# Low halves of sixteen weight blocks made early, stored, and loaded by casting transfers

## The chip, the core and the metric

The kernel runs on one NeuronCore of a Trainium2 chip. Five engines with queues of their own work side by side: TensorE (PE, with its weight loads shown as PEld) multiplies, VectorE (DVE) and ScalarE (ACT) do elementwise work, GpSimd (POOL) issues the indirect and the casting transfers, and SyncE (SP) issues the plain ones. The metric is device time in microseconds (us) of one execution.

## The reference

One decoder layer for 512 prompt rows and 64 sample rows (576 in all) of width 1024:

```
z  = rmsnorm(x) @ w_in                      # q, k, v, su, sv, gate_a, gate_b
A  = windowed attention(q, k, v);  B = gelu(su) * spatial_gate(layernorm(gelu(sv)))
h  = sigmoid(gate_a) * (A @ w_branch_a) + sigmoid(gate_b) * (B @ w_branch_b)
x1 = x + h @ w_out
x2 = x1 + peer(rmsnorm(x1))                 # 128*128 experts, 8 heads, top 16 each
x3 = x2 + sigmoid(rmsnorm(x2) @ w_ple_gate) * (p @ w_ple)

peer: q = xb @ w_q; scores against two sets of 128 keys; top 16 of each, top 16 of their sums
      out = sum over the 16 experts of a head: softmax gate * gelu(u[idx] . xb) * v[idx]
```

## The kernel before

**Split products.** Products run in fp32r. Each 128x1024 weight block is loaded in fp32 (`w_raw`), ACT rounds it into a high half (`w_hi`, line 66), DVE subtracts to get the low half (`w_lo`, line 67), and PE sums three products for each 128 rows of depth (`tform`, line 82): high by high, high by low of the activations, low by high. So a block is 24 matmuls. `load_block` (line 69) does this for every block, with four raw buffers and three of each half.

**Stages.** 30 blocks of `w_in` with attention and the gating unit beside them; the branch products (8 blocks `w_br`) and the output product (8 blocks `w_out`); 16 blocks of the retrieval queries (`peer_wq`) with the key scores; then the experts. The 16384 experts are handled in two ways. For 384 of the 576 rows the kernel multiplies by all experts in 128 first-stage blocks (`stage1`: `peer_uT[j]`, 24 matmuls of 384 columns, then gelu) and 128 second-stage blocks (`stage2`: `peer_v`, 18 matmuls of 512 columns), with a dense matrix of gates that `build_g` makes from one-hot products. For the other 192 rows (64 sample rows and 128 prompt rows) it gathers each chosen expert's row of u and v by an indirect transfer on POOL's queue (`gather_row`, line 721) and lets DVE multiply (lines 733 and 740): 384 rows in all, into five buffers (`row`).

**Retrieval.** `retrieve` is a generator of DVE steps (top 16, decoding of positions), run for five groups of rows. Groups 0 and 1 give the indices of the gathers; group 2 is the first that `build_g` needs, by way of `make_ew` (line 797), which transposes its results on PE (line 799). While groups 0 to 2 are retrieved, first-stage blocks are put between the steps, up to `S1_TOPK` = 4, 9 and 13 blocks in all. Then the loop over `tb` (24 times 16 tokens) brings the blocks up to a goal, calls `make_ew` for group 2 at `tb` 0, and runs `build_g`. In the loop over j the remaining first-stage blocks run between second-stage blocks; `SPILL`, the even blocks 2 to 38, have their results parked in DRAM and read back.

**Pace of the gathers.** `pay` adds a credit per step and gathers a row for each whole credit: 0.5 for a first-stage block during retrieval, 2.0 or 3.5 for a `tb`, 1.65 for a first-stage block in the loop over j, and `G2` (1.6 while first-stage blocks are left, then 2.0) for each j. At j = 112 the first 128 must be done, and at j = 122 (`TAIL1`) all that are left are issued.

**What sets the order.** The program text gives priorities. A planner of the framework walks the program with estimated durations, lets every engine take the ready instruction of highest priority, and so fixes each engine's order before the run; on the chip each engine keeps that order and waits by semaphores. `high_priority` lifts the splits of weights ahead of other work. An instruction that waits for a buffer or a result holds everything behind it on its engine or its queue.

```python
    for ti in range(3):
        for _ in retrieve(ti, ti < 2):
            if len(acts) < S1_TOPK[ti]:
                stage1()
        ...
        while len(acts) < goal:
            stage1()
        if tb == 0:
            make_ew(*found[2])
        build_g(tb)
```

Of the kernel before, what the change touches and what calls it, by code (L numbers as in the profile page):

```python
# [7 lines left out]
F32 = mybir.dt.float32  # L8
# [9 lines left out]
P = 128  # L18
# [3 lines left out]
KC = 8  # L22
# [9 lines left out]
ONE = (1, 2)  # L32
TAIL0 = 112
TAIL1 = 122
S1_TOPK = (4, 9, 13)
TBK = 7
S1_END = 6
RING = 44
# [2 lines left out]
TILES = [(512, 64), (0, 128), (128, 128), (256, 128), (384, 128)]  # L41
HALVES = (slice(0, 256), slice(256, 576))
EPS = 1e-6
STARTS = [0, 16, 24, 29, 33, 36, 38, 40, 42, 43, 44, 45, 46, 47, 48, 49]


@with_exitstack
def tile_decoder_step(ctx: ExitStack, tc: tile.TileContext, a, o):
# [20 lines left out]
    def load_block(src, shape=(P, KC, P), urgent=True):  # L69
# [5 lines left out]
            split(raw, hi, lo)  # L75
        return hi, lo

    def tform(ps, w, x, wk=0, nk=KC):
        n, i = 3 * nk, 0
        for k in range(nk):  # L80
            for wi, xi in ((0, 0), (0, 1), (1, 0)):
                mark_pe[0] = T.matmul(ps, lhsT=w[wi][:, wk + k, :], rhs=x[xi][k], start=i == 0,  # L82
                                   stop=i == n - 1)
                i += 1
# [15 lines left out]
    x1d = dr.tile([KC, P, NB], F32, name="x1d")  # L100
    pld = dr.tile([NT, D], F32, name="pld")
    ad = dr.tile([NSP, P, NB], F32, name="ad")
    gd = dr.tile([NJ // JB, P, NB // TB, JB, TB], F32, name="gd")

    psBs = ExitStack()
# [385 lines left out]
    for g in range(4):  # L491
        split(suT[:, g, :], mh[:, g, :], ml[:, g, :])
    e2s.close()
    ple(TILES[:3])
    ahl = [[t[:, g, :] for g in range(4)] for t in (ah, al)]
    mhl = [[t[:, g, :] for g in range(4)] for t in (mh, ml)]
    hs = ([], [])
    for c in range(KC):
        w = load_block(a["w_br"][c])
        for i, (x, k0_) in enumerate(((ahl, 0), (mhl, 4))):  # L500
            sg = sgs[2 * c + i]
            joint(w, x, lambda ps, cols: V.tensor_tensor(sg[:, cols], sg[:, cols], ps, op=ALU.mult), k0_, 4,
                  (mm, lambda: bank("sc"))[i])
        ga = tt()
        V.tensor_tensor(ga, sgs[2 * c], sgs[2 * c + 1], op=ALU.add)
        if c % 4 == 0:
            h4 = [f4(F32R), f4(F32R)]
        for h, t in zip(hs, h4):
            h.append(t[:, c % 4, :])
        split(ga, hs[0][c], hs[1][c])  # L510

    gp = pool(ctx, "gp", 2)
    rows = ExitStack()
    rowp = pool(rows, "rowp", 5)

    def row(shape=(P, D), dt=F32):
        return rowp.tile(list(shape), dt, name="row")

    x1 = f8(f4)
    xg = (f8(x4), f8(x4))  # L520
# [1 line left out]
    for c in range(KC):  # L522
        w = load_block(a["w_out"][c])
        xc = tt()
        S.dma_start(xc, a["xT"][c])
        joint(w, hs, lambda ps, cols: V.tensor_tensor(x1[c][:, cols], ps, xc[:, cols], op=ALU.add))
        S.dma_start(x1d[c], x1[c][:, P:512])
        gcol = vecs[:, 8 + c:9 + c]
        A.activation(xg[0][c], x1[c], AF.Copy, scale=gcol)
        V.scalar_tensor_tensor(xg[1][c], x1[c], gcol, xg[0][c].bitcast(F32), op0=ALU.mult, op1=ALU.subtract)  # L530
        if c:
            add(c - 1, x1[c - 1])
# [243 lines left out]
    def stage1():  # L776
        nonlocal j1, nlive
        j = j1
        j1 += 1
        w = load_block(a["peer_uT"][j])  # L780
        ps = (mm() if j % 2 or phase[0] > 1 else bank("pv"))[:, :NB]
        tform(ps, w, xb)
        if j in SPILL:
            act = held_x[-1][:, sorted(SPILL).index(j) % 6, :]
        else:
            n = nlive % RING
            nlive += 1
            act = held_x[n // 6][:, n % 6, :] if n < NXP - 6 else (
                acp[0][:, n - NXP + 6, :] if n < RING - 6 else held_x[-1][:, n - RING + 6, :])
        A.activation(act, ps, AF.Gelu_apprx_tanh)  # L790
        acts[j] = act
        if j in SPILL:
            S.dma_start(ad[sorted(SPILL).index(j)], act)
        pay(GP[phase[0]])
# [57 lines left out]
    for tb in range(NB // TB):  # L852
        if tb == TBK:
            for i, r_ in enumerate(rest_t):
                for _ in r_:
                    pass
                make_ew(*found[5 - len(rest_t) + i])
            tks.close()
            late = pool(aLs, "aL", 1, "right")
            acp.append(late.tile([P, RING - NXP, NB], F32, name="aL"))  # L860
            g0 = late.tile([P, JB, TB], F32, name="g0")
        if tb < TBK:
            goal = S1_TOPK[2] + (tb + 1) * (S1_PRE - S1_TOPK[2]) // TBK
        else:
            goal = S1_PRE + (tb - TBK + 1) * (NSP + RING - 1 - S1_END - S1_PRE) // (NB // TB - TBK)
        while len(acts) < goal:
            stage1()
        if tb == 0:
            make_ew(*found[2])
        build_g(tb)  # L870
        for _ in range(2):
            if rest_t and next(rest_t[0], 1) == 1:
                rest_t.pop(0)
                make_ew(*found[4 - len(rest_t)])
        pay(GT[tb >= TBK] if tb < 22 else 0)
# [79 lines left out]
    for j in range(NJ):  # L955
        for jb in (2, 4) if j == 0 else (j + 4,):
            if jb in SPILL:
                back[jb] = d3.tile([P, NB], F32, name="x1c")
                S.dma_start(back[jb], ad[sorted(SPILL).index(jb)])
        if j and j - 1 not in SPILL and j1 < NJ:  # L960
            stage1()
        pay(G2[0] if j1 < NJ else G2[1])
        if j == TAIL0:
            aLs.close()
            xds.close()
            spp.append(pool(sps, "spare", 2, "right"))
            gather(max(0, P - done[0]), mark_pe[0])
            pg = gp.tile([P, D], F32, name="xr")
            S.dma_start(pg, a["ple_g"])
            tails.append(gathered(0))  # L970
        if j == TAIL1:
            gather(1000, mark_pe[0])
        if j == NJ - 2:
            tails.append(gathered(1))
        if j % JB == 0:
            gsl = gsp[(j // JB + 1) % 2].tile([P, NB // TB, JB, TB], F32, name="gs")
            nb = NB // TB if j else NB // TB - 1
            with tc.high_priority(offset=0 if j else 300):
                S.dma_start(gsl[:, :nb], gd[j // JB][:, :nb])
            if j == 0:  # L980
                A.activation(gsl[:, nb], g0, AF.Copy)
        vw = load_block(pv_view[j], (P, D))
        wf = acts.pop(j)
        if j in SPILL:
            wf = back.pop(j)
        wfv = wf.rearrange("p (b t) -> p b t", t=TB)
        V.tensor_tensor(wfv, wfv, gsl[:, :, j % JB, :], op=ALU.mult)
        wh = d2.tile([P, NB], F32R, name="wh")
        wl = d2.tile([P, NB], F32R, name="wl")
        split(wf, wh, wl)  # L990
        held.append((j, wh, wl, *vw))
        if j != NJ - 2:
            for t in range(3):
                for hj in held:
                    stage2(t, *hj)
            held.clear()
        if max(SPILL) < j <= max(SPILL) + KC:
            add_x1(j - max(SPILL) - 1)
# [150 lines left out]
```

## Time and profile before

| what | us |
|---|---|
| median of three runs | 1764.56 |
| these runs | 1764.26 to 1765.45 |
| the profiled execution | 1767.91 |
| its span, first to last instruction | 1766.1 |
| PE busy in the span | 1741.2 |
| DVE busy | 1436.6 |
| ACT busy | 868.3 |
| POOL busy | 518.3 |

In the profile, busy times are counted in one execution. A PE that is busy all the time tells that its queue never ran dry, so what can be gained is in the gaps and in stretches of lower clock. An idle time carries the name of what ended it. The granted clock is given as a share of full speed; the two levels are 2.4 GHz and 1.2 GHz, so a mean of 0.83 over a stretch says that a third of it ran at the lower one.

### The profile page before, as it was taken

How to read it: one execution, taken by the hardware profiler on the slowest of the kernel's cores; microseconds unless marked ns; L12 is line 12 of the kernel's file. 1: busy time of each engine (PE TensorE's matmuls, PEld its weight loads, DVE VectorE, ACT ScalarE, POOL GpSimd, SP SyncE). 2: the span in 40 equal slices, each digit the busy share in tenths (PEclk: the TensorE clock that was granted, in tenths of full speed). 3: DMA queues.
4: the chain of work that ended last, by engine and by line, in shares of the span. 5: the costliest groups of instructions: out<-in, count | busy, mean ns of one | idle time of the engine just before them, and what ended most of it. 6: DMA issues, size and time to landing. Idle time of an engine off the chain costs nothing.

```text
span 1766.1 us, 27818 instructions
## 1 busy us (share of the span) xinstructions
PE 1741.2 (99%) x10118; PEld 1574.5 (89%) x10118; DVE 1436.6 (81%) x2878; ACT 868.3 (49%) x1526; POOL 518.3 (29%) x390
## 2 busy tenths in 40 slices
PE   8999999999999899999999999999999999999999
PEld 8987999999999899999988888899999899887777
DVE  6355556549899999999898899998888888999963
ACT  6567443344335698998833333333333333333441
POOL 0000000000002112455245454454544544566300
PEclk9999999999999999999999999999999999999999
DMA  7211224443227577999999999999999999999832
GB/s 238 93 49 48 72 93 135 142 151 97 81 92 235 170 245 238 361 350 349 345 397 359 374 393 405 395 410 361 364 333 365 361 340 325 340 375 375 289 127 78
DMA packets 176601, 457.07 MB, mean 259 GB/s; under 512 B 15568, under 2 KB 77008, under 8 KB 174416
## 3 DMA queue, kind: packets, MB, share of 16 engines
q1 hardware_dynamic: 120880, 253.22, 40.9%
q0 software_dynamic: 55584, 202.07, 30.8%
q8 instruction: 79, 1.29, 0.3%
q14 instruction: 58, 0.48, 0.1%
HBM read 420.18 MB, written 35.78 MB: 258 GB/s over the span
## 4 chain that ended last, share of the span: by engine, by line
PE 81%; issue 6%; DVE 5%; DMA 4%; POOL 3%; ACT 1%; SPq 0%; POOLq 0%; DVEq 0%; ACTq 0%
PE mm L82 36%; PE oacc L951 24%; PE pv L82 5%; POOL row L721 3%; PE oacc L916 2%; PE sc L836 2%; PE pt L836 2%; DMA row<-peer_u,idx 2%; DMA row<-peer_v,idx 2%; PE sc L82 1%; DVE w_lo L67 1%; PE sc L594 1%; PE pv L461 1%; PE mm L916 1%; PE pv L329 1%
## 5 line engine op out<-in xcount | busy, mean ns | idle before, releaser
L66 ACT ACTIVATE w_hi<-w_raw 128x1024 fp32r<-128x1024 f32 x325 | 344.0, 1059 | 367.9 <-PE mm L82 265.5
L721 POOL DMA_INDIRECT row<-peer_u,idx x192 | 260.2, 1355 | 861.6 <-issue 515.2
L67 DVE TENSOR_TENSOR w_lo<-w_raw,w_hi 128x1024 fp32r<-128x1024 f32 x325 | 396.6, 1221 | 80.1 <-ACT w_hi L66 77.2
L82 PE MATMUL mm<-xd,w_hi 128*128 128x384 f32 x1552 | 405.7, 340 | 0.5 <-ACT w_hi L66 0.5
L721 POOL DMA_INDIRECT row<-peer_v,idx x192 | 256.6, 1337 | 240.5 <-DVE acc L740 215.2
L82 PE MATMUL mm<-x,w_hi 128*128 128x320 f32 (+1 forms) x1504 | 305.4, 297 | 0.0
L82 PEld LDWEIGHTS mm<-xd,w_hi 128*128 128x128 f32 x1552 | 281.3, 189 | 6.0 <-ACT w_hi L66 0.8
L82 PE MATMUL mm<-xd,w_lo 128*128 128x384 f32 x776 | 263.8, 340 | 1.6 <-DVE w_lo L67 1.6
L82 PEld LDWEIGHTS mm<-x,w_hi 128*128 128x128 f32 x1504 | 239.3, 188 | 12.5 <-issue 9.0
L740 DVE SCALAR_TENSOR_TENSOR acc<-row,wts,acc 128x1024 f32<-128x1024 f32 x192 | 245.7, 1279 | 2.1 <-DMA row<-peer_v,idx 1.6
L951 PE MATMUL oacc<-w_hi,wl 128*128 128x512 f32 x768 | 241.5, 396 | 2.3 <-DVE wl L67 2.3
L951 PE MATMUL oacc<-w_hi,wh 128*128 128x512 f32 x768 | 242.0, 395 | 1.3 <-ACT wh L66 1.3
L733 DVE SCALAR_TENSOR_TENSOR row<-row,xr 128x1024 f32<-128x1024 f32 x192 | 231.5, 1219 | 12.5 <-DMA row<-peer_u,idx 12.4
L951 PE MATMUL oacc<-w_lo,wh 128*128 128x512 f32 x768 | 241.5, 395 | 0.0
L82 PE MATMUL mm<-x,w_lo 128*128 128x320 f32 (+1 forms) x752 | 220.6, 294 | 0.0
L951 PEld LDWEIGHTS oacc<-w_hi,wl 128*128 128x128 f32 x768 | 144.1, 188 | 37.7 <-DVE wl L67 3.1
L951 PEld LDWEIGHTS oacc<-w_lo,wh 128*128 128x128 f32 x768 | 144.3, 188 | 34.5
L951 PEld LDWEIGHTS oacc<-w_hi,wh 128*128 128x128 f32 x768 | 143.5, 188 | 31.0 <-ACT wh L66 1.6
L82 PEld LDWEIGHTS mm<-xd,w_lo 128*128 128x128 f32 x776 | 146.7, 189 | 2.3 <-DVE w_lo L67 2.2
L82 PEld LDWEIGHTS mm<-x,w_lo 128*128 128x128 f32 x752 | 141.1, 188 | 1.1 <-issue 0.8
L82 PE MATMUL pv<-xd,w_hi 128*128 128x384 f32 x496 | 136.5, 347 | 0.7 <-ACT x L790 0.7
L66 ACT ACTIVATE wh<-x 128x384 fp32r<-128x384 f32 x66 | 34.7, 526 | 162.0 <-PE oacc L951 152.7
(326 smaller groups left out, 2383.4 us busy)
## 6 DMA issues: line engine op xcount, KB each, us to landing
w_raw<-peer_uT SPq DMA_DIRECT2D x128, 512.0 KB
w_raw<-peer_v SPq DMA_DIRECT2D x128, 512.0 KB
gd<-gs SPq DMA_DIRECT2D x24, 1024.0 KB
gs<-gd SPq DMA_DIRECT2D x15, 1536.0 KB
w_raw<-w_in SPq DMA_DIRECT2D x30, 512.0 KB
w_raw<-peer_wq SPq DMA_DIRECT2D x16, 512.0 KB
w_raw<-w_br SPq DMA_DIRECT2D x8, 512.0 KB
w_raw<-w_out SPq DMA_DIRECT2D x8, 512.0 KB
```

The source lines that it names most:

```text
L66: A.activation(hi, src, AF.Copy)
L67: V.tensor_sub(lo, src, hi.bitcast(F32))
L82: mark_pe[0] = T.matmul(ps, lhsT=w[wi][:, wk + k, :], rhs=x[xi][k], start=i == 0, stop=i == n - 1)
L329: T.matmul(pvs[pr, :], lhsT=vt[:, t0 + j, pr], rhs=pT, start=j == 0, stop=j == nk // P - 1)
L461: T.matmul(ps[:r], lhsT=xi[:, k, :r], rhs=wl_[k][wi][:, hh * 512:(hh + 1) * 512], start=i == 0, stop=i == 5)
L594: T.matmul(ps[:, b * P:(b + 1) * P], lhsT=qp[:, b * P:(b + 1) * P], rhs=sk, start=True, stop=True)
L721: ins = G.indirect_dma_start(out=row_, out_offset=None, in_=table, in_offset=bass.IndirectOffsetOnAxis(ap=ix, axis=0))
L733: V.scalar_tensor_tensor(row_, row_, 1.0, xrs[ti], op0=ALU.mult, op1=ALU.mult, accum_out=dots[:, s:s + 1])
L740: V.scalar_tensor_tensor(accs[ti], row_, wts[:, s:s + 1], accs[ti], op0=ALU.mult, op1=ALU.add)
L836: T.matmul(pt[:, t * P:(t + 1) * P], lhsT=oa[:, t, :], rhs=ob[:, t, :], start=True, stop=True)
L916: T.matmul(p[:r, :hs.stop - hs.start], lhsT=xi[:, k, :r], rhs=w[k][wi][:, hs], start=k == 0 and xi is xh and wi == 0, stop=k == KC - 1 and ...
L951: mark_pe[0] = T.matmul(oacc[t][hh], lhsT=wi[:, ts], rhs=vi[:, hh * 512:(hh + 1) * 512], start=j == 0 and last == 0 and vi is vh, stop=j = ...
```

## The change

For the first 16 first-stage blocks (`PRE`) the low half is made earlier. The row pools are opened before the branch products. `low_ahead`, called once ahead of `ple`, once in each of the 8 branch blocks and once in each of the 8 output blocks, loads one block of `peer_uT` by POOL's queue into a row buffer, and for the block loaded by the call before it lets ACT round and DVE subtract in fp32, and stores the low half to DRAM (`wsd`) by POOL's queue. Later `load_low` takes the place of `load_block` for these blocks: SP loads the raw block, ACT rounds the high half as before, and POOL's queue loads the low half with a transfer that casts fp32 to fp32r. Three settings change too: `S1_TOPK` is 4, 10, 15; `make_ew` for group 2 stands two blocks ahead of the goal of `tb` 0; and up to j = 38 the pace `G2` is 1.4 in place of 1.6.

```diff
-S1_TOPK = (4, 9, 13)
+S1_TOPK = (4, 10, 15)
+PRE = 16
...
+    def load_low(j):
+        raw = wp.tile([P, KC, P], F32, name="w_raw", bufs=4)
+        S.dma_start(raw, a["peer_uT"][j])
+        hi = wp.tile([P, KC, P], F32R, name="w_hi", bufs=3)
+        lo = wp.tile([P, KC, P], F32R, name="w_lo", bufs=3)
+        G.dma_start(lo.rearrange("p k c -> p (k c)"), wsd[j])
+        with tc.high_priority(offset=1000):
+            A.activation(hi, raw, AF.Copy)
+        return hi, lo
...
+    wsd = dr.tile([PRE, P, D], F32, name="wsd")
...
     e2s.close()
+    gp = pool(ctx, "gp", 2)
+    rows = ExitStack()
+    rowp = pool(rows, "rowp", 5)
+
+    def row(shape=(P, D), dt=F32):
+        return rowp.tile(list(shape), dt, name="row")
+
+    raws = []
+
+    def low_ahead(n):
+        for _ in range(n):
+            j = len(raws)
+            if j < PRE:
+                raws.append(row())
+                G.dma_start(raws[j], a["peer_uT"][j].rearrange("p k c -> p (k c)"))
+            if j - 1 in range(PRE):
+                raw, hi = raws[j - 1], row(dt=F32R)
+                A.activation(hi, raw, AF.Copy)
+                V.tensor_sub(raw, raw, hi.bitcast(F32))
+                G.dma_start(wsd[j - 1], raw)
+                if j == PRE:
+                    raws.append(None)
+
+    low_ahead(1)
     ple(TILES[:3])
...
             joint(w, x, lambda ps, cols: V.tensor_tensor(sg[:, cols], sg[:, cols], ps, op=ALU.mult), k0_, 4,
                   (mm, lambda: bank("sc"))[i])
+        low_ahead(1)
...
         joint(w, hs, lambda ps, cols: V.tensor_tensor(x1[c][:, cols], ps, xc[:, cols], op=ALU.add))
+        low_ahead(1)
...
-        w = load_block(a["peer_uT"][j])
+        w = load_low(j) if j < PRE else load_block(a["peer_uT"][j])
...
         while len(acts) < goal:
+            if tb == 0 and len(acts) == goal - 2:
+                make_ew(*found[2])
             stage1()
-        if tb == 0:
-            make_ew(*found[2])
...
-        pay(G2[0] if j1 < NJ else G2[1])
+        pay((G2[0] if j > max(SPILL) else 1.4) if j1 < NJ else G2[1])
```

## Rows read from the trace of the kernel before

**Rows 1.** Page: busy us, share of the span, instructions of each engine.

```profile
PE 1741.2 (99%) x10118; PEld 1574.5 (89%) x10118; DVE 1436.6 (81%) x2878; ACT 868.3 (49%) x1526; POOL 518.3 (29%) x390
```

**Rows 2.** Waits of PE: who, for what, us in total, times, longest.

```profile
PE pt L799 <- DVE e L672: 3.2, 1, 3.2
PE oacc L951 <- DVE wl L67: 2.3, 2, 1.6
PE mm L82 <- DVE w_lo L67: 1.6, 2, 1.0
PE sc L836 <- DVE ob L827: 1.5, 2, 0.8
PE oacc L951 <- ACT wh L66: 1.3, 1, 1.3
...
PE sc L836 <- DVE best L640: 0.7, 1, 0.7
PE mm L82 <- ACT w_hi L66: 0.5, 1, 0.5
PE pv L82 <- DVE w_lo L67: 0.5, 1, 0.5
```

**Rows 3.** Windows: length, busy PE, PEld, DVE, ACT, POOL, clock, DMA share, GB/s.

```profile
262.00:321.00 59.00, 58.96 (x418) 56.28 (x416) 39.73 (x66) 22.61 (x32) 0.00 (x0) 1.00 0.37 122
321.00:372.00 51.00, 51.00 (x387) 50.88 (x386) 26.96 (x39) 17.88 (x23) 0.00 (x0) 1.00 0.49 152
...
580.00:590.00 10.00, 8.50 (x39) 7.86 (x38) 10.00 (x23) 7.85 (x10) 0.00 (x0) 0.83 0.56 190
590.00:600.00 10.00, 7.39 (x43) 7.07 (x41) 10.00 (x31) 6.14 (x8) 1.68 (x1) 1.00 0.43 142
600.00:610.00 10.00, 9.37 (x54) 9.11 (x54) 8.84 (x34) 6.65 (x18) 1.68 (x1) 0.83 0.52 195
...
1100.00:1140.00 40.00, 37.74 (x183) 32.41 (x182) 36.42 (x58) 13.29 (x18) 18.17 (x15) 1.00 1.00 396
```

**Rows 4.** PE's timeline around the first and the last block ahead of make_ew.

```profile
508.67 0.62 PE L82 MATMUL pv<-xd,w_hi 128*128 128x384 f32 x2
...
600.63 0.47 PE L799 MATMUL pt<-c_ident,e 128*128 128x128 f32 x1 [3.24 <-DVE e L672]
```

**Rows 5.** Chain of waits, 508 to 541 us: start, us, what.

```profile
513.10 4.16 PE mm L82 x24
...
540.08 5.07 DMA row<-peer_u,idx
```

**Rows 6.** Tile w_lo, 508 to 600.63 us: count, ns min/median/max, first to last start.

```profile
L82 PE MATMUL pv<-xd,w_lo x80: 332/336/443, 509.1 to 592.9; 128*128 128x384 f32 x80
...
L82 PE MATMUL mm<-xd,w_lo x80: 332/336/550, 513.3 to 597.1; 128*128 128x384 f32 x80
L67 DVE TENSOR_TENSOR w_lo<-w_raw,w_hi x20: 1206/1217/1226, 507.0 to 597.5; 128x1024 fp32r<-128x1024 f32 x20
```

**Rows 7.** DVE's timeline at one low half: start, us, [idle before].

```profile
514.20 1.21 DVE L67 TENSOR_TENSOR w_lo<-w_raw,w_hi 128x1024 fp32r<-128x1024 f32 x1
515.33 0.08 DVE L611 MATCH_VALUE_LOAD tix<-top,sc 128x8 f32 x1
```

**Rows 8.** DVE's timeline just ahead of a wait of PE in the loop over j.

```profile
1109.93 1.23 DVE L733 SCALAR_TENSOR_TENSOR row<-row,xr 128x1024 f32<-128x1024 f32 x1 [1.50 <-DMA row<-peer_u,idx]
```

**Rows 9.** ACT's timeline in the branch products.

```profile
315.23 1.06 ACT L66 ACTIVATE w_hi<-w_raw 128x1024 fp32r<-128x1024 f32 x1 [4.24 <-PE sc L82]
```

**Rows 10.** POOL's timeline during the retrieval, in brackets the time it was held.

```profile
553.60 1.67 POOL L721 DMA_INDIRECT row<-peer_u,idx  x1 [5.60 <-DVE row L733]
562.82 1.68 POOL L721 DMA_INDIRECT row<-peer_u,idx  x1 [7.55 <-DVE row L733]
576.29 1.68 POOL L721 DMA_INDIRECT row<-peer_u,idx  x1 [11.79 <-DVE row L733]
```

**Rows 11.** Tile row, 508 to 600.63 us: columns as for tile w_lo.

```profile
L721 POOL DMA_INDIRECT row<-peer_u,idx x10: 934/1020/1683, 540.1 to 594.5; - x10
```

More of the change, by code (lines that the diff above doesn't have):

```diff
@@ L510, in tile_decoder_step @@
         split(ga, hs[0][c], hs[1][c])
[L512 to L517, printed above, removed]
     x1 = f8(f4)
```

## The prediction

> **What bounds the kernel now.** I read the page's busy times first: PE is busy 1741.2 of 1766.1 us [rows 1], so no other engine can be made faster to any use unless PE was waiting for it. Next I read the waits of PE. All that bear on this change are short; the longest is 3.2 us [rows 2]. The third view is the windows. In the branch and output products PE hardly pauses (58.96 of 59 us, 51 of 51); between 580 and 600 us it is busy for 8.50 and 7.39 of 10 us while DVE is busy for all 10, and the granted clock falls to 0.83 twice, in 580 to 590 and in 600 to 610 [rows 3]. So DVE ends the waits there. The place is the end of the retrieval: PE has nothing left in its order but `make_ew`, which waits for the last DVE step of group 2 (line 672) until 600.63 [rows 4].
>
> How late is that? A first-stage block takes 4.16 us when nothing holds it [rows 5]. Ahead of `make_ew` PE did 80 + 80 matmuls with a low half, 8 to a block, so 20 blocks [rows 6], beginning at 508.67 [rows 4]. Dense, they end at 508.67 + 20 x 4.16 = 591.9. DVE's result came 8.7 us after that. In the waits, 3.2 of it is `make_ew` and 1.6 + 0.5 + 0.5 are halves of weights that came late [rows 2]; the clock of 0.83 in 580 to 590 costs 10 x 0.17 = 1.7 [rows 3]; about 1.2 shows in no row of waits. The dip after it, in 600 to 610, costs 1.7 more. So 10.4 us lie at the retrieval. Further on, DVE holds PE 1.5 + 0.7 in the gate stage and 2.3 in the loop over j, and ACT holds it 1.3 [rows 2]. All of it together is 16.2 us; with nothing else added, a profiled run could not come below 1767.9 - 16.2 = 1751.7.
>
> **Taken from DVE in the retrieval.** Of the 20 low halves in that stretch [rows 6] the first, at 507.0, belongs to the second block (the first block's was made before 508). So those of blocks 2 to 15, 14 of them, leave the 92 us. DVE's next instruction starts 1.13 us after such a start [rows 7], so 14 x 1.13 = 15.8 us, which no other engine does there. DVE's result for group 2 would be ready at 600.6 - 15.8 = 584.8.
>
> That does not mean that PE gains 8.7 us, since PE's place for `make_ew` moves too. The program text has 13 + 2 blocks ahead of it, yet PE did 20 [rows 6]: the planner filled in blocks until it thought that group 2 was ready, between the 19th and the 20th block's end (587.7 to 591.9). The chip was 8.7 us or more later than this plan. What makes DVE late against the plan must be mostly the many short steps of the top 16, since the low halves are few and regular; and these steps stay. If so, the plan of the changed kernel puts group 2 at about 572 to 576 (15.8 earlier), behind 15 or 16 blocks, and PE arrives at 508.67 + 16 x 4.16 = 575.2 and waits for 584.8. I take the lateness to shrink with the DVE work that it is spread over: 8.7 x (92 - 15.8) / 92 = 7.2, a gain of **1.5 us**. The bounds are 10.4 (all of it, both dips of the clock too) and -2 (half a block of bad luck in where the planner cuts). The new order of `make_ew`, two blocks ahead of the goal, and the goals of 10 and 15 only say which blocks stand where; their matmuls are the same, and I give them nothing. The one more gather in this stage costs DVE one row step of about the price of a low half, 1.2 us, and is within that bound.
>
> **Gate stage.** What DVE no longer does before 585 leaves the stretch from there to the loop over j 16 us more to fit the same DVE work into. The 1.5 and 0.7 us for which PE waits for DVE there [rows 2] should go: **2.2 us**, bounds 0 and 3.5 (with ACT's 1.3).
>
> **Loop over j.** 39 steps at 1.4 in place of 1.6 are 7.8 gathers fewer up to j = 38; they come later. Each is 512 KB on transfer engines that are at a share of 1.00 [rows 3], and 1.2 us on DVE. The waits of PE there are for a low half of the activations (`wl`, 2.3 us in two times [rows 2]) that sits behind a row step which had waited 1.50 us for its row [rows 8]. About 4 MB less at 396 GB/s [rows 3] is 10 us less transfer time in that stage, so I count **2.3 us** won, bounds 0 and 2.7. The gathers put off: by the credits, before, the 384th row was issued at j = 119; now the last is issued at 122, with `TAIL1`, and its result is used at j = 126. No new wait, by this count.
>
> **Added in the branch and output products.** 16 roundings at 1.06 us on ACT [rows 9] and 16 subtractions at 1.2 us on DVE, into 59 + 51 us in which DVE is busy 67 and ACT 40, and in which transfers take 0.37 to 0.49 of the engines' time [rows 3]. The 32 new transfers are 16.8 MB, 153 GB/s more beside the 122 to 152. POOL has nothing else there. What hides it is that PE's banks are emptied with room to spare: ACT stood idle 4.24 us before a block's rounding [rows 9]. Cost **0**; if the cover is gone it is the rival below. No row here shows a store by POOL; the nearest is a gather's 5.07 us from issue to landing [rows 5].
>
> **Casting loads.** 16 issues by POOL in the retrieval at 1.7 us each [rows 10], 27 us on an engine that is idle then. A block's low half can be asked for when PE has finished the third block before it, so there are two blocks, 8.3 us, for issue and flight, against 5.07 for a plain gather on the same queue [rows 5]. No row shows a cast of this size alone: bounds 0 and the rival below. A DVE step no longer frees the raw buffer, ACT does, which can only help SP's loads.
>
> Sum: 1.5 + 2.2 + 2.3 = **6.0 us**. A profiled run goes from 1767.9 to 1761.9; the median of the runs is 3.3 below the profiled one, so 1764.56 - 6.0 = **1758.6**. Own range of this case: 1755 to 1763.5.
>
> The rows show POOL held in its order: the gathers of the retrieval waited 5.60, 7.55 and 11.79 us for DVE to free a row [rows 10]. The Trainium skill (DMA: Bandwidth & Descriptors, Anatomy of one DMA) says that a semaphore wait happens on the issuing sequencer before dispatch, never in the transfer engine. The trace agrees, and by that rule a casting load behind such a gather stands still with it: the second rival below.
>
> **Rivals.**
>
> *Full relief.* The planner leaves 18 blocks or more ahead of `make_ew`, or the lateness came with the low halves. PE is then at 508.67 + 18 x 4.16 = 583.6 when the result is ready at 584.8. Gain 10.4 - 1 at the retrieval, with the other two 14: **1750.6**. For it: PE's waits there for halves of weights, 2.6 us in sum. Against it: the 3.2 us for line 672, which is no low half.
>
> *Casting loads late (slower).* POOL's order has a casting load behind a gather that DVE holds up. The slack of a load is 8.3 - 5.1 = 3.2 us. Holds like those [rows 10] would stop PE for 2.4 + 4.4 + 8.6 = 15.4 us; 7.2 of this lies beside the wait for group 2 that stays anyway, so 8.2 are new, less 2.3 from the loop over j: +5.9 against before, **1770.5**. It decides from a hold of 3.2 us on. For it: three holds of that size. Against it: the planner places a gather only where it thinks a row is free, and its error is bounded by the same 8.7 us.
>
> *No relief.* The freed DVE time is filled with row steps that the planner pulls forward: ten gathers were issued by 600 us [rows 11], where the program text has four at that point. Then only the loop over j gains: **1762.3**.
>
> *Store loop.* A rounding may wait for a row buffer whose store is in flight: 1.06 + 1.2 + 5.07 = 7.3 us a round, against 51 / 8 = 6.4 us for an output block: 0.9 x 8 = 7 us lost: **1765.6**. Against it: five buffers where four are in use.
>
> **How the numbers follow.** A measurement of this kernel can tell some 0.2%, 3.5 us, from no change. My forecast has a chance of 0.45 (of this 0.07 gain less than 3.5), full relief 0.25, late loads 0.15 (0.02 of it ends within 3.5), no relief 0.10 (all but 0.02 within), store loop 0.05 (0.02 of it within). Faster: 0.38 + 0.25 + 0.02 = 0.65. Same: 0.07 + 0.02 + 0.08 + 0.02 = 0.19. Slower: 0.13 + 0.03 = 0.16. The range goes from 1749, just under full relief, to 1768, which takes in the store loop and the milder late loads.
>
> **What would show it.** Right: PE's wait at line 799 stays at some microseconds, now about 15 us earlier and behind 15 to 17 blocks; the waits for `w_lo` in the retrieval are gone; no wait for `wl` in the loop over j; nothing new before 508 us. Full relief shows as no wait at line 799 and no dip of the clock. Late loads show as PE waiting for the transfer `w_lo<-wsd`, with POOL held by a row step ahead of it. The store loop shows as block periods over 6.4 us in the output products. I would be wrong most simply if the planner's error does not stay with the top 16 steps.

## The result

| | median us | ratio to before, 95% interval |
|---|---|---|
| before | 1765.0 | |
| after | 1777.8 | 1.0068 [1.0058, 1.0079] |

The change makes the kernel 12.8 us slower. The forecast was 1758.6 with a range of 1749 to 1768, so both the sign and the range were wrong.

I read the profile after in the same order as the one before. The first view is the page's span, with its busy times: busy us, share of the span, instructions of each engine.

```profile
span 1777.2 us, 27935 instructions
...
PE 1745.0 (98%) x10118; PEld 1580.2 (89%) x10118; DVE 1435.0 (81%) x2878; ACT 883.9 (50%) x1542; POOL 555.0 (31%) x438
```

PE does the same 10118 matmuls as in [rows 1]. The span is 11.1 us longer: 7.3 of it is more idle time of PE (32.2 against 24.9), 3.8 is the same matmuls taking longer. Next, the waits of PE (who, for what, us in total, times, longest):

```profile
...
PE mm L93 <- DVE w_lo L68: 5.1, 3, 3.8
PE pt L830 <- DVE e L703: 3.8, 1, 3.8
PE sc L867 <- DVE ob L858: 3.1, 2, 1.8
PE mm L93 <- DVE c L538: 3.0, 1, 3.0
PE sc L867 <- ACT oa L856: 2.4, 1, 2.4
PE oacc L982 <- DVE wl L68: 1.4, 1, 1.4
PE mm L93 <- ACT w_hi L67: 0.9, 1, 0.9
```

Against [rows 2] the wait for the evicted bank of the branch products (line 538, where DVE empties it) is new, and one wait for a low half is 3.8 us long, where the longest was 1.0. The windows (length, busy PE, PEld, DVE, ACT, POOL, clock, DMA share, GB/s) put both in their place:

```profile
262.00:321.00 59.00, 53.70 (x358) 49.85 (x357) 46.93 (x67) 33.45 (x45) 12.08 (x23) 0.97 0.88 303
321.00:372.00 51.00, 51.00 (x387) 50.88 (x386) 30.27 (x47) 18.01 (x23) 0.00 (x0) 1.00 0.56 184
...
1100.00:1140.00 40.00, 36.18 (x159) 31.20 (x158) 32.74 (x54) 11.96 (x16) 13.76 (x11) 0.91 0.99 382
```

In the branch products PE was busy 58.96 of 59 us [rows 3]; now it is busy 53.70 at a clock of 0.97, and transfers take 0.88 of their engines' time in place of 0.37. In the output products PE is as busy as before. In the loop over j the clock, 1.00 before [rows 3], is 0.91. Laid out by PE's first matmul of each stage, the 11.1 us of the two profiled executions are:

| stage | before us | after us | difference |
|---|---|---|---|
| start to the end of the input products | 261.9 | 261.1 | -0.7 |
| branch products | 59.6 | 67.8 | +8.2 |
| output products, to the first retrieval query | 59.6 | 60.2 | +0.6 |
| from there to the first first-stage block | 127.6 | 128.5 | +0.9 |
| retrieval and gate stage, to round 1 of the loop over j (rounds count from 0) | 377.8 | 374.0 | -3.8 |
| rounds 1 to 36 | 221.9 | 221.9 | 0.0 |
| rounds 36 to 40 | 28.6 | 32.4 | +3.8 |
| rounds 40 to 112 | 496.3 | 496.3 | 0.0 |
| round 112 to the end | 133.0 | 135.0 | +2.0 |

**The branch products.** Of the 8.2 us, 5.3 are idle time of PE and 3.0 the same matmuls taking longer. The idle time of ACT between 262 and 321 us was mostly ended by PE before (first line); in after two kinds are there that before has not:

```profile
ACT w_hi L66 <- PE sc L82: 24.1, 7, 4.2
```

```profile
ACT row L523 <- DMA row<-peer_uT: 8.6, 4, 4.8
ACT row L523 <- DMA wsd<-row: 8.1, 3, 4.0
```

The rounding of line 523 waits for its row to be loaded, or for a row buffer whose store is in flight. The longest such wait, in the timelines of ACT, DVE and PE (start, us, what, in brackets the idle time before):

```profile
303.76 1.06 ACT L523 ACTIVATE row<-row 128x1024 fp32r<-128x1024 f32 x1 [4.79 <-DMA row<-peer_uT]
304.73 1.04 ACT L67 ACTIVATE w_hi<-w_raw 128x1024 fp32r<-128x1024 f32 x1
305.68 0.67 ACT L67 ACTIVATE c<-t 128x576 fp32r<-128x576 f32 x1
```

```profile
304.86 1.22 DVE L524 TENSOR_TENSOR row<-row 128x1024 f32<-128x1024 f32 x1 [2.22 <-ACT row L523]
306.00 1.22 DVE L68 TENSOR_TENSOR w_lo<-w_raw,w_hi 128x1024 fp32r<-128x1024 f32 x1
307.13 0.75 DVE L68 TENSOR_TENSOR c<-t,c 128x576 fp32r<-128x576 f32 x1
307.80 0.81 DVE L538 TENSOR_TENSOR c<-c,mm 128x256 f32<-128x256 f32 x2
```

```profile
308.36 0.47 PE L93 MATMUL mm<-x,w_hi 128*128 128x256 f32 x2 [3.03 <-DVE c L538]
```

This is to be read downwards. ACT stands 4.79 us on a load of the making; the weight halves of the products and the halves of `c` come behind it in ACT's order; DVE then stands on ACT; the bank is emptied at 307.80, and PE has waited 3.03 us for it. Two more waits of PE, 0.93 and 1.06 us, stand at the stage's first block (265.03 and 266.60), behind a rounding at 259.20 that had waited 2.93 us for its load.

**The loop over j.** DVE's and PE's timelines at the other loss:

```profile
1117.51 0.55 DVE L68 TENSOR_TENSOR wl<-aL,wh 128x384 fp32r<-128x384 f32 x1
1124.09 1.03 DVE L1018 TENSOR_TENSOR x<-x,gs 128x384 f32<-128x384 f32 x2 [6.03 <-DMA gs<-gd]
1125.04 1.22 DVE L68 TENSOR_TENSOR w_lo<-w_raw,w_hi 128x1024 fp32r<-128x1024 f32 x1
```

```profile
1126.31 0.69 PE L93 MATMUL mm<-xd,w_lo 128*128 128x384 f32 x1 [3.82 <-DVE w_lo L68]
```

Two gate products (line 1018) stand on DVE in front of a weight's low half and wait 6.03 us for a gate slice of 1.5 MB. The products are far ahead of their use: half of the 128 rounds have theirs by then, while PE is in round 38. The load of the slice (SP's timeline, after and before) is asked for 5.4 us ahead of round 36 in after, 7.3 us behind its start in before:

```profile
1108.18 0.33 SPq L1010 DMA_DIRECT2D gs<-gd  x1
```

```profile
1115.62 0.33 SPq L979 DMA_DIRECT2D gs<-gd  x1
```

### The profile page after: what moved, and what is told of

It is laid out like the page before. It is cut to its first block, busy times and chain, and to the rows that moved or that the text cites. A ratio compares the mean times of both kernels' runs of the same rounds, so it can differ in the third digit from the quotient of the medians.

```text
span 1777.2 us, 27935 instructions
## 1 busy us (share of the span) xinstructions
PE 1745.0 (98%) x10118; PEld 1580.2 (89%) x10118; DVE 1435.0 (81%) x2878; ACT 883.9 (50%) x1542; POOL 555.0 (31%) x438
## 4 chain that ended last, share of the span: by engine, by line
PE 77%; DVE 7%; issue 6%; DMA 5%; POOL 3%; ACT 1%; SPq 0%; POOLq 0%; DVEq 0%; ACTq 0%
PE mm L93 37%; PE oacc L982 23%; PE pv L93 4%; POOL row L752 3%; DMA row<-peer_v,idx 2%; PE oacc L947 2%; PE sc L867 2%; PE pt L867 2%; DMA gs<-gd 1%; DMA wsd<-row 1%; DVE w_lo L68 1%; PE mm L947 1%; PE pv L341 1%; PE sc L625 1%; PE sc L323 1%
## 5 line engine op out<-in xcount | busy, mean ns | idle before, releaser
L67 ACT ACTIVATE w_hi<-w_raw 128x1024 fp32r<-128x1024 f32 x309 | 327.2, 1060 | 336.3 <-PE mm L93 273.1
L68 DVE TENSOR_TENSOR w_lo<-w_raw,w_hi 128x1024 fp32r<-128x1024 f32 x309 | 377.1, 1221 | 85.8 <-ACT w_hi L67 84.9
L752 POOL DMA_INDIRECT row<-peer_v,idx x192 | 270.8, 1410 | 242.7 <-DVE acc L771 217.9
L93 PE MATMUL mm<-x,w_hi 128*128 128x256 f32 (+1 forms) x1504 | 307.8, 299 | 4.0 <-DVE c L538 3.0
```

The source lines that it names most:

```text
L67: A.activation(hi, src, AF.Copy)
L68: V.tensor_sub(lo, src, hi.bitcast(F32))
L752: ins = G.indirect_dma_start(out=row_, out_offset=None, in_=table, in_offset=bass.IndirectOffsetOnAxis(ap=ix, axis=0))
```

## Experiments

Ratios are to before, with runs of before on the same chip. E1 to E4, E5 to E8 and so on ran together. A difference of two medians from different groups is good to a us or so, since before itself moved between 1764.9 and 1766.5.

**What the making costs.** Theory: it costs through its transfers, which hold ACT. Rival: through its arithmetic on ACT and DVE. E3 leaves the making out; the casting loads read the full weights, so low halves and result are not the reference's.

```diff
-        for _ in range(n):
+        for _ in range(0):
-        G.dma_start(lo.rearrange("p k c -> p (k c)"), wsd[j])
+        G.dma_start(lo, a["peer_uT"][j])
```

> The changed kernel without making the low halves: nothing is loaded, split or stored in the branch and output products, and the casting loads read the blocks of peer_uT themselves (so the low halves are not those of the reference). Theory A (the making holds ScalarE and with it the branch products, 9.0 us up to the first first-stage block): this kernel reaches that block at about 508.7 us as before does, and takes about 1777.8 - 9.0 = 1768.8. Theory B (the loss comes with the casting loads and what follows): about 1777, with the first block at 508.7 and the loss behind it.

Measured 1769.4, 1.0023 [1.0012, 1.0034]: 8.4 us under after (9.0 when each is taken against its own runs of before), as theory A had it, and the branch products take 59.6 us again. E8 keeps the sixteen roundings and subtractions and leaves out their transfers:

```diff
-                raws.append(row())
-                G.dma_start(raws[j], a["peer_uT"][j].rearrange("p k c -> p (k c)"))
+                raws.append(raws[0] if raws else row())
+                if j == 0:
+                    G.dma_start(raws[j], a["peer_uT"][j].rearrange("p k c -> p (k c)"))
...
-                V.tensor_sub(raw, raw, hi.bitcast(F32))
-                G.dma_start(wsd[j - 1], raw)
+                V.tensor_sub(row(), raw, hi.bitcast(F32))
```

> The kernel after with the arithmetic of the making alone: one row is loaded once and rounded and subtracted sixteen times, nothing is stored, and the casting loads read the full weights in place of the stored low halves, so the low halves (and with them the result) are not the reference's. Theory A (ScalarE is held by the making's transfers, not by its roundings): the branch products end within 2 us of before, and the time is 1769 to 1771 us. Theory B (the sixteen roundings and subtractions take ScalarE and VectorE from the branch products): the branch products end some 8 us late again, and the time is 1776 to 1779 us.

Measured 1768.7, 1.0014 [1.0004, 1.0024], no more than E3. The arithmetic is free, even bunched into 45 us (246.9 to 291.9): the window of 262 to 321 us shows PE busy throughout, with ACT at 31 us:

```profile
262.00:321.00 59.00, 59.00 (x419) 56.55 (x418) 49.97 (x76) 31.08 (x42) 0.00 (x0) 1.00 0.40 132
```

E5 keeps all of the making and only spreads it: each rounding is ordered behind the last matmul that stands before it in the program's text. This tie (`after`, of the kind `NoSync`) binds the planner's order; it adds no semaphore.

```diff
-                A.activation(hi, raw, AF.Copy)
+                after(A.activation(hi, raw, AF.Copy), mark_pe[0])
```

> The kernel after, with one edit: each rounding of the making is ordered behind the TensorE instruction that was traced just before it, so that the sixteen makings can't be bunched into the branch products and spread over branch and output products, one for each block. Theory A (the loss of some 8 us in the branch products comes from the bunching: ScalarE, in its fixed order, waits for the making's loads and row buffers): the block stages lose at most 2 us against before and the time is about 1770 us (1768 to 1773). Theory B (the load itself, one rounding of 1.06 us and one subtraction of 1.13 us a block on engines that also split the products' own weights, costs the time wherever it stands): the loss stays, spread over both stages, and the time stays at about 1777 us (1775 to 1780).

Measured 1773.6, 1.0041 [1.0028, 1.0055], between the two theories: half of the cost is back, 4.2 us by the medians. The tile `row` (count, ns min/median/max, first to last start) first in after, then in E5:

```profile
L525 POOL DMA_DIRECT2D wsd<-row x16: 533/538/538, 250.6 to 320.3; - x16
```

```profile
L525 POOL DMA_DIRECT2D wsd<-row x16: 533/538/538, 280.7 to 375.6; - x16
```

In after the planner ran the sixteen rounds of the making in 70 us, 4.6 us apart, far ahead of the blocks they were written beside; in E5 they are 6.3 us apart. No load or store of the making holds ACT between 262 and 321 us in E5, and branch and output products together take no longer than in E3. Between the output products and the first block E5's trace takes 2.9 us longer than before; 1.1 of it is work that only changed sides (twelve small matmuls, `sc<-ones,rstd`, stand ahead of that boundary in before and behind it in E5), 1.27 is one wait of PE for ACT (`qp`), the rest I have no row for. So the theory holds for the branch products, and the rival falls. Nor is it the crowd on the transfer engines alone: with all its transfers kept, at DMA shares of 0.65 (262 to 321 us) and 0.92 (321 to 372), E5 keeps PE busy for 58.96 of 59 and 51.00 of 51 us. Where the rest of E5's median goes is open; its profiled execution took 1769.95, 3.6 us less than the median.

**What the casting loads give.** E4 is after with the sixteen blocks split in the retrieval as before.

```diff
-        w = load_low(j) if j < PRE else load_block(a["peer_uT"][j])
+        w = load_block(a["peer_uT"][j])
```

> The changed kernel with the making kept, but with the first 16 first-stage blocks loaded and split as before, so the stored halves are not used. Theory A: the first first-stage block begins at about 517.7 us as in the changed kernel, and nothing is won behind it: 1777.8 + 3.8 = 1781.6. Theory B (the loss needs the casting loads): the first block at about 509 and a time near 1766.

Measured 1781.7, 1.0096 [1.0077, 1.0116], 3.9 us over after. This difference is not clean: in E4's trace the branch products lose 9.4 us, 1.2 more than in after, the input products take 2.1 us longer than in after's, and from the first block to round 1 it takes 376.3 us against after's 374.0. By that stretch of these two traces the loads are worth 2.3 us; over all traces it is 3.6 (see the part on the prediction).

**What the order gives.** E2 is before with the goals of 10 and 15 blocks and the early `make_ew` alone.

```diff
-S1_TOPK = (4, 9, 13)
+S1_TOPK = (4, 10, 15)
...
+            if tb == 0 and len(acts) == goal - 2:
+                make_ew(*found[2])
             stage1()
-        if tb == 0:
-            make_ew(*found[2])
```

> The kernel before with the new goals (4, 10, 15) and make_ew two blocks ahead of the goal, nothing else. Theory A (order alone is worth nothing, the gain of the retrieval is the freed VectorE): within 2 us of before, with about 20 blocks ahead of make_ew and its wait still near 600 us. Theory B (the order carries the gain): 3 to 4 us faster, about 1761.

Measured 1767.5, 1.0010 [0.9998, 1.0021]: no difference that can be told, as theory A had it.

**What the pace costs.** E1 is before with the pace of 1.4 and nothing else.

```diff
-        pay(G2[0] if j1 < NJ else G2[1])
+        pay((G2[0] if j > max(SPILL) else 1.4) if j1 < NJ else G2[1])
```

> The kernel before with one edit: the pace of 1.4 up to j = 38. Theory A (the pace costs in the loop over j: the changed kernel lost 3.8 us between j = 36 and j = 40, in a wait of 3.8 us with a dip of the clock, and 2.0 us after j = 112, though it gathers less there): 3 to 6 us slower than before, about 1769, with a wait of VectorE for the gate slice (gs<-gd) of some 6 us near j = 37. Theory B (the pace wins 2.3 us as the prediction had it, and the loss in the loop came with the other edits): about 1762.5.

Measured 1772.2, 1.0041 [1.0028, 1.0054]: 6.7 us lost where I had forecast 2.3 gained. DVE's waits in the loop show the product behind its slice in E1 too, and PE's waits there a low half behind it:

```profile
DVE x L987 <- DMA gs<-gd: 8.6, 2, 6.5
DVE row L733 <- DMA row<-peer_u,idx: 3.1, 3, 1.9
```

```profile
PE mm L82 <- DVE w_lo L67: 4.2, 1, 4.2
```

E11 goes the other way, to 1.8 on the first part of the loop, on top of E7 (below; 1764.6 at 1.6):

```diff
-        pay(G2[0] if j1 < NJ else G2[1])
+        pay((G2[0] if j > max(SPILL) else 1.8) if j1 < NJ else G2[1])
```

> The kernel with the spread making, the new order and the casting loads (1764.6 us at pace 1.6) with the pace of the loop's first part raised to 1.8 in place of the change's 1.4. Theory A (more gathers ahead keep products from being put ahead of their gate slice; the loop's loss falls with the pace): 1761 to 1765 us, with no wait of VectorE on a gate slice over 1 us. Theory B (a pace above 1.6 brings the row sums in VectorE's way of the weights' low halves, as the prediction held): 1766 to 1770 us.

Measured 1776.0, 1.0056 [1.0040, 1.0071], slower than either theory. Rounds 36 to 40 take 25.8 us, so the loss there is gone, but rounds 1 to 36 take 232.8 in place of 221.9. DVE's waits in the loop are now for rows, and PE waits for low halves of the activations behind them:

```profile
DVE row L764 <- DMA row<-peer_u,idx: 15.4, 15, 3.9
...
DVE acc L771 <- DMA row<-peer_v,idx: 7.1, 5, 2.7
DVE x L1018 <- DMA gs<-gd: 3.8, 2, 3.0
```

So 1.6 lies between two losses. Is the one at 1.4 the products that run ahead? E6 ordered each product behind the last matmul that stands before it in the text:

```diff
-        V.tensor_tensor(wfv, wfv, gsl[:, :, j % JB, :], op=ALU.mult)
+        after(V.tensor_tensor(wfv, wfv, gsl[:, :, j % JB, :], op=ALU.mult), mark_pe[0])
```

> The kernel before with the lower pace of 1.4 in the loop's first part, and the gate products of the loop ordered behind the TensorE instruction traced just before them, so that they can't be put far ahead on VectorE. Theory A (the 6.7 us that the lower pace cost came from gate products that were put ahead and held VectorE while the gate slice was still in flight): the waits of the product on the gate slice, 8.6 us in all with the lower pace alone, are gone, and the time is 1763 to 1767 us. Theory B (the lower pace itself costs: gathers that are put off collide later, with the tail): about 1772 us (1770 to 1774), with the loss behind block 100 of the loop.

Measured 1906.4, 1.0795 [1.0778, 1.0812]: inconclusive. The wait for slices went (0.5 us), but each product now came too late by itself: PE waits for `wh` 48 times, 46.9 us. E9 gives the products two rounds of room:

```diff
+        marks.append(mark_pe[0])
+        pr = V.tensor_tensor(wfv, wfv, gsl[:, :, j % JB, :], op=ALU.mult)
+        if j > 1:
+            after(pr, marks[-3])
```

> The kernel before with the lower pace of 1.4, and each gate product of the loop held behind the TensorE instruction that was traced two rounds earlier, so that it can run at most two rounds (some 17 us) ahead of its use and doesn't come late for it either (held behind the same round's, it came late by itself and gave 1906 us). Theory A (the lower pace costs because products put far ahead hold VectorE while their gate slice is in flight): VectorE's wait for the gate slice, 8.6 us in two waits with the lower pace alone, is under 1 us, and the time is 1765 to 1768 us. Theory B (the lower pace costs by something else, such as the gathers that it puts off): the time stays at 1771 to 1773 us even though the wait is gone.

Measured 1787.8, 1.0123 [1.0106, 1.0140]. The total fits neither theory, but the trace splits it: rounds 36 to 40 take 25.8 us, against 32.4 in E1 and 28.6 in before, so the loss there is gone; from round 85 to the end 23 us are lost. E10 is the same bound on E7.

> The kernel with the spread making, the new order, the casting loads and the old pace of 1.6 (1764.6 us), with the gate products held to two rounds ahead as well. It kept 2.1 us of VectorE's wait for gate slices and one stall of TensorE of 1.62 us at 1126. Theory A (these are the same product-ahead wait, in small): 1761 to 1764 us. Theory B (nothing of the end hangs on them): 1764 to 1766 us; should the bound itself delay products, more.

Measured 1781.9, 1.0096 [1.0080, 1.0113]: 17 us are lost from round 85 on. E13 sets the bound only while first-stage blocks are left (`if j > 1 and j1 < NJ`), with the pace of 1.4; E16 is the same bound at the old pace.

> The kernel before with the lower pace of 1.4 and the bound of two rounds on the gate products in the loop's first part alone, up to the last first-stage block. With the bound on the whole loop the first part ended 2 us ahead of before (with the pace alone 7 us behind it) and the second part lost 23 us to products that came late. Theory A (the pace's loss is products put ahead of their gate slice in the first part, and the bound there takes it out): VectorE waits for no gate slice in the first part, and the time is 1763 to 1766 us. Theory B (the pace loses by the gathers that it puts off, or the bound costs in the second part even where it isn't set): 1769 us or more, with the loss behind round 85 of the loop.

> The kernel before with the bound of two rounds on the gate products in the loop's first part and nothing else. Theory A (before's own loop loses a little to products put ahead: VectorE's 1.2 us on a gate slice and TensorE's 1.63 us at 1128.69): 1763 to 1765 us, 1 to 2 us under before. Theory B (the product-ahead wait is the lower pace's alone): 1765 to 1767 us.

Measured 1786.5, 1.0117 [1.0102, 1.0133], as theory B had it, and 1781.0, 1.0088 [1.0074, 1.0102], outside both. In both, rounds 36 to 40 take 25.8 us, and 22 and 13 us are lost from round 85 to the end (in E16 4.5 more between rounds 40 and 85). The windows of the two parts of the loop (881 to 1517, 1517 to 1700), for before, E16 and E13, columns as above:

```profile
881.00:1517.00 636.00, 633.48 (x3139) 563.82 (x3140) 564.33 (x735) 224.36 (x303) 315.22 (x242) 1.00 0.97 369
1517.00:1700.00 183.00, 182.09 (x787) 145.52 (x786) 161.36 (x163) 70.68 (x97) 92.89 (x67) 1.00 0.88 322
```

```profile
881.00:1517.00 636.00, 633.65 (x3132) 563.56 (x3132) 548.74 (x708) 224.07 (x302) 316.75 (x239) 1.00 0.96 361
1517.00:1700.00 183.00, 174.40 (x732) 136.55 (x731) 168.53 (x182) 65.78 (x91) 96.31 (x70) 0.98 0.91 340
```

```profile
881.00:1517.00 636.00, 635.73 (x3152) 565.81 (x3151) 541.27 (x703) 225.78 (x304) 314.12 (x232) 1.00 0.96 355
1517.00:1700.00 183.00, 166.44 (x689) 129.08 (x687) 169.04 (x177) 60.99 (x83) 113.93 (x77) 0.98 0.95 355
```

DVE does 735 instructions in the first part of before, 708 with the bound, 703 with the bound and the lower pace; what is not done there is done in the second part, where DVE was busy 161 of 183 us already. I read this so: products that run ahead, and gathers paid early, are DVE work done where there is room. With the bound on, the lower pace costs another 5.5 us (E13 against E16), by the traces behind round 112; without the bound that stretch loses 1.7 us to it (below). Two more kernels put the bound on E12 (below), at 1.6 (E14) and 1.4 (E15):

> The kernel with the spread making, the casting loads, the old order and the old pace (1762.6 us) with the bound of two rounds on the gate products in the loop's first part. Theory A (the stall of TensorE near 1126 us, a low half or a product behind a gate slice, is left in small at pace 1.6): 1760 to 1762.5 us. Theory B (nothing is left there): within 1 us of 1762.6 us.

> The kernel with the spread making, the casting loads and the old order, with the change's pace of 1.4 and the bound of two rounds on the gate products in the first part. Theory A (with the products bounded, the lower pace does what the prediction held, fewer row sums in front of the weights' low halves): 1759 to 1762 us, under the same kernel at 1.6. Theory B (with products bounded the pace is neutral, and later gathers cost in the tail): 1762 to 1766 us.

Measured 1776.6, 1.0064 [1.0050, 1.0078], and 1781.4, 1.0096 [1.0080, 1.0111]: the bound loses again, and 1.4 is 4.8 us behind 1.6. Neither fits a theory. Last, E17 (on E1) and E18 (on E5) were to hold only the products of rounds 72 to 79, which I had taken for those of the slice waited for:

```diff
+        if 72 <= j < 80:
+            after(pr, marks[38])
```

> The kernel before with the lower pace of 1.4, and only the eight products of the tenth gate slice (rounds 72 to 79) held behind the first-stage block of round 38; with the pace alone they stood on VectorE some 36 rounds ahead of their use and waited 6.5 us for that slice. All other products may run ahead as before. Theory A (this one wait is most of what the pace costs): VectorE's wait for the slice is under 1.5 us, TensorE's stall of 4.2 us there is gone, and the time is 1767 to 1769.5 us. Theory B (the pace costs by the row sums that it puts off into the loop's second part): 1771 to 1774 us even without the stall.

> The kernel after with the making spread (1773.6 us) and the products of rounds 72 to 79 held behind the first-stage block of round 38; the pace stays 1.4. Theory A (the stall there, 3.4 us, is the loop's loss): 1769 to 1770.5 us. Theory B (the stall only moves to another slice or round): 1773 to 1775 us.

Measured 1771.8, 1.0040 [1.0026, 1.0054], and 1772.3, 1.0038 [1.0024, 1.0051]. These say nothing on the theories: DVE's order in E17 is that of E1, in E18 that of E5, instruction by instruction, and the wait is still there (6.1 us in E17). Exactly 64 products stand ahead of the one that waits, so by count it is one of rounds 64 to 71, and the hold came behind it.

**Both losses out.** E7 is after with the spread making and the old pace, E12 the same with the old order too.

```diff
-                A.activation(hi, raw, AF.Copy)
+                after(A.activation(hi, raw, AF.Copy), mark_pe[0])
...
-        pay((G2[0] if j > max(SPILL) else 1.4) if j1 < NJ else G2[1])
+        pay(G2[0] if j1 < NJ else G2[1])
```

> The kernel after with the making spread as in the paced making and the old pace of 1.6 in the loop: the two losses found so far taken out, the casting loads and the new order kept. Theory A (both losses stand by themselves, the casting loads gain some 4 us): 1777.8 - 8.4 + (0 to 8.4) for what the spread making still costs - 6.7 = 1763 to 1767 us, at or below before. Theory B (neither is recovered: the making costs through its load, and the loop's loss comes from having been brought forward): 1773 to 1778 us.

> The kernel with the spread making, the casting loads and the old pace (1764.6 us), with the old order of the retrieval: 9 and 13 first-stage blocks ahead of the top lists, and the first softmax transposes behind all blocks of the first gate stretch. Theory A (the new order uses what the casting loads free; alone it gave nothing): 1766 to 1768 us, the gain gone. Theory B (the casting loads gain by themselves, the order is neutral): 1764 to 1765.5 us.

Measured 1764.6, 0.9988 [0.9979, 0.9996], and 1762.6, 0.9979 [0.9970, 0.9987]. E7 is as theory A had it, E12 a little under both of its theories. E12 is the version to keep: casting loads and spread making, nothing else, 3.2 us under before. The two intervals overlap, so whether the new order costs anything there is open. PE's waits in E12 that lie in the retrieval and gate stage:

```profile
PE sc L867 <- DVE ob L858: 5.2, 3, 2.3
PE pt L830 <- DVE e L703: 3.8, 1, 3.8
...
PE sc L867 <- ACT oa L856: 0.3, 1, 0.3
```

## Why the prediction was wrong, step by step

**Retrieval and gate stage, 3.7 us: the sum held, by two errors that cancel.** The trace has 3.8. Over all traces this stretch takes 375.9 to 378.8 us in the nine kernels without the casting loads and 370.2 to 375.5 in the eleven with them (means 377.3 and 373.7), in the old order as in the new, so the gain is the loads' and of the forecast size. `make_ew` stands behind 15 blocks, as forecast, and its wait stays (3.8 us, [rows 2] had 3.2); the waits for weight halves in the retrieval are gone. But the terms were wrong. DVE's result for group 2 comes 66.5 us behind the first block in place of 92.0, which is 25.5 earlier where 14 low halves gave 15.8. Those 92.0 us held 19 low halves, and in after none stands ahead of the result: 14 are not made there any more, and the other five, of blocks 17 to 21, come behind it. 19 x 1.13 = 21.5; the rest is one row sum, some short steps and 2 us of idle time of DVE. So PE is 66.5 - 15 x 4.16 = 4.1 us late there in place of 8.8, a gain of 4.7 where I had 1.5 (and my arrival at 575.2 with the result at 584.8 would have been 9.6 us late, not 7.2). Behind it 0.9 us were lost where I had 2.2 gained: PE waits 5.5 us for DVE and ACT in the gate stage.

**Casting loads, 0 us: right.** No wait of PE names `w_lo<-wsd`, so the rival of late loads falls. POOL's timeline (in brackets the time it was held):

```profile
539.07 0.53 POOL L84 DMA_DIRECT2D w_lo<-wsd  x1 [3.63 <-PE pv L93]
542.78 1.00 POOL L752 DMA_INDIRECT row<-peer_u,idx  x1 [3.19 <-DVE c L670]
543.77 0.59 POOL L84 DMA_DIRECT2D w_lo<-wsd  x1
```

The loads are held by PE's use of the buffers, block by block, and the gather between them delays the next load by 0.54 us against the 4.16 of a block, not by a hold like [rows 10]. The Trainium skill (DMA: Bandwidth & Descriptors, Anatomy of one DMA) has such waits on the issuing sequencer; the trace agrees, since the load stands behind the gather, but the rule found nothing to cost here.

**Making, 0 us: the step that failed first.** The wrong sentence is "What hides it is that PE's banks are emptied with room to spare", drawn from ACT's 4.24 us of idle time [rows 9]. Idle time of ACT and DVE does hide the arithmetic (E8). But I had only put a price on instructions, and had taken the place in the program's text for the place in time. Nothing tied the making to the products, so the planner ran it at 4.6 us a round, twelve of the sixteen in the branch products, at a DMA share of 0.88; and an instruction that waits for such a transfer holds everything behind it in ACT's order. Measured: 8.4 us (E3), of which spreading gives back 4.2 (E5). My store-loop rival had this mechanism, a rounding that waits for a row buffer in flight, but in the output products, where nothing was lost, at 7 us and with a chance of 0.05.

**Loop over j, 2.3 us gained: the second step that failed.** The lower pace costs 6.7 us (E1). The two waits for `wl` did go from the first part of the loop (the row sum of [rows 8] stood ahead of the smaller one, 0.62 us), and so did the 4 MB: in rounds 1 to 36 of E1 transfers fell from 386 to 366 GB/s. But those rounds take 221.9 us either way, and around the wait, between 1100 and 1140 us, the share is still 0.99 in after. I had priced the transfers saved and not what DVE would do in place of the row sums. It does gate products: when round 36 begins, 64 of them are done at the pace of 1.4 (after, E1, E5, E17), 61 at 1.6 (before, E7, E12) and 59 at 1.8 (E11). Each eighth frees a slice and asks for the next 1.5 MB; the slice is asked for earlier, and DVE waits for it in front of a low half. Where the products are bounded this loss is gone (E9, E13). At the other end, 360 of the 384 row sums are done at round 112 in E1, 368 in before. Six traces at 1.4 (after, E1, E3, E4, E5, E8) stand against four at 1.6 (before, E2, E7, E12): rounds 36 to 40 take 31.0 to 32.4 us against 26.7 to 28.6, round 112 to the end 133.5 to 135.0 against 132.0 to 133.0. On average that is 4.3 + 1.7 = 6.0 of the 6.7 us. That the end loses by the row sums put off is argued from their number; no run tests it alone.

**The sum.** Making 8.4 and pace 6.7, less 3.6 for the casting loads, make 11.5 against 12.8 measured; the new order, 1.9 by E2's median and not to be told from nothing, would make it 13.4.

## What to carry to other kernels

Work that is "hidden in idle time" is hidden only if its waits are too: ask of each added instruction what it will wait for, and what stands behind it on its engine; and if a planner orders the work, tie the added rounds to the work that is to cover them. A pace that feeds two kinds of work to one engine can't be lowered for one without seeing what takes its place, and work run ahead may be a store for a later stretch that has no room: look at that stretch before bounding it.

## What the runs showed of the hardware

A plain load or store of 512 KB took POOL 0.53 us to issue, a gather of the same size 0.95 to 2.0 us in the retrieval of after; a casting load took 0.53 us too, where I had counted 1.7. In E5, with the making spread at a DMA share of 0.65 in the branch products, a 512 KB store of POOL's landed 3.0 us after its issue and a load 6.2 us (medians of seven each). In after, a wait of PE of 3 to 4 us came with a stretch at the lower of the two clock levels: the granted clock was 0.97 over the 59 us (262 to 321) that hold the 3.03 us, and 0.91 over the 40 us (1100 to 1140) that hold the 3.82. By these shares that is work of 1.8 and 3.6 us; of the latter 2.2 show as longer matmuls (PE busy 26.3 us of rounds 36 to 40 before, 28.6 after).
